# Order of transposes, loads, weight differences and normalisations at the seams of a one-core transformer block

## The chip, the cores and the metric

The kernel runs on one core of a Trainium2 chip. Its engines are TensorE (PE, matrix products; PEld is its weight load), VectorE (DVE), ScalarE (ACT), GpSimd (POOL) and SyncE (SP), whose queue issues nearly all DMAs. The metric is the device time of one execution in microseconds (us), the median of the runs.

## The reference, cut

One block on x (2048 x 1024): a mixer (a recurrent half and a gated half, normalised, times `w_out`), then a feed-forward part with a causal convolution of width 3. Both are wrapped in RMS norms and modulated by six vectors made from c.

```python
mod = c_act @ w_ada[l] + b_ada[l]
sh_m, sc_m, gt_m, sh_f, sc_f, gt_f = split(mod, 6)
h = rmsnorm(x, g_mix_pre) * (1 + sc_m) + sh_m
lru_x, lru_gate, g_u, g_v = split(h @ w_in)
y = concat([rmsnorm(y_lru, g_lru_out), rmsnorm(y_gmlp, g_gmlp_out)])
y = y @ w_out
x = x + gt_m * rmsnorm(y, g_mix_post)
h = rmsnorm(x, g_ffn_pre) * (1 + sc_f) + sh_f
up = causal_depthwise_conv(h @ w_up, ffn_conv_w, ffn_conv_b)
g_ff, v_ff = split(up, 2)
y = (gelu(g_ff) * v_ff) @ w_down
x = x + gt_f * rmsnorm(y, g_ffn_post)
```

## The kernel before

Features lie on the 128 partitions, positions on the free axis. A float32 operand is split into a rounded part (`split`, L136 or L140, a cast) and the rest (L141, a subtraction on DVE); a product is three matmuls of 128x512 (`mm3`, L177 to L179).

**Mixer.** It goes over four chunks of 512 positions: `mixer_z` (products with `w_in`; `v_proj` is its part for `v`), `mixer_norm` (squares on ACT, sums on POOL and DVE, then `rms_bcast`: two matmuls with a matrix of ones, `rl0_m` and `rg0_m` for chunk 0, that add over the partitions; their operand `rl0_hl` is split on DVE), `mixer_out` (product with `w_out`; `oo` is the copy of a result from its bank), `mixer_post`. The vectors of modulation 2 to 5 are made beside it by `ada_task`: DVE sums eight products into `ada_m`, eight transposes on PE turn it, and a reduction on DVE makes a column of each.

**Order.** Background work is written as generators in the list `bg`; each `tick()` in the main loops takes every one a step further, `drain` runs one to its end. A scheduler then orders each engine's instructions by priorities (`tc.high_priority`) and by when tiles come free. Tiles come from pools: `tp` (tag `t4`, 36 tiles), `wp` (`w`, 8), `rw` (`wraw`, 4, raw weights), `lp` (`ld`, 3, loads), `rp` (6). The mixer has its own accumulation banks; those of the feed-forward part, `pf`, take their place when the mixer's last copies are done.

**Feed-forward.** It has two halves C of 1024 positions. `up_phase` runs 24 column blocks f. From f = 2 of C = 0 on, a block is formed from seven products (`up_pair`, `PIECES` 11, t1, t2, 21, 22, t3, t4), each of an operand of `H2` (among them the sums s1 to s4 of four quarters of h, made by `h2_sums`; `hs4` is the split of s4) with a weight piece (a quarter of the block or a difference of quarters). One period of f is 84 matmuls. `up_weights` loads two raw tiles, `wug` and `wuv`, makes the differences on POOL and splits each into a piece; in C = 0 they are also stored to `wkd`, from where C = 1 loads them for f from 2 on. So 22 blocks of C = 0 and two of C = 1 make differences on the chip. `late_chunks` finishes chunks 2 and 3 beside the first up phase. `down(C, t)` multiplies with `w_down` and sums over f in eight banks, one for each d; `evict` squares and copies a bank; `final` normalises with `fr` and adds x2:

```python
t = lp.tile([P, 2, 4, P], F32, tag="ld", name=f"wt{n}")
t2, t1 = t[:, 0], t[:, 1]
w["11"] = piece(b11, f"w11_{n}")
pool.tensor_tensor(out=t1, in0=b12, in1=b11, op=ALU.subtract)
w["t1"] = piece(t1, f"wt1_{n}")
```

`final` of (0,0) runs inside `down(0, 1)`, that of (0,1) at f = 1 of the second up phase, that of (1,0) inside `down(1, 1)`, and that of (1,1) ends the kernel, with its results added to a copy of x2 in DRAM by four accumulating DMAs from POOL.

Of the kernel before, what the change touches and what calls it, by code (L numbers as in the profile page):

```python
# [40 lines left out]
def block_kernel(ctx: ExitStack, tc: tile.TileContext, xt, cols, rows, wada, wada_r, win_k, win_s, win_v, wgate, wsp, wout, wup, wdown, out):  # L41
# [506 lines left out]
    def mixer_out(c, late=False):  # L548
# [690 lines left out]
```

## Time and profile before

| | before |
|---|---|
| median of 3 runs | 2196.03 us (2190.37 to 2196.96) |
| profiled execution | 2193.87 us |
| its span | 2192.1 us |
| mean granted PE clock | 0.975 of full speed |
| PE busy | 2065.3 us, 94% |
| DVE busy | 1427.9 us, 65% |
| ACT busy | 928.2 us, 42% |
| POOL busy | 438.6 us, 20% |
| DMA | 229 GB/s over the span |

The span goes from the first to the last recorded instruction or transfer of the profiled execution; its own time is 1.8 us longer. Busy shares are means over all stages. The idle time in front of an instruction, with what ended it, stands in the timeline in square brackets; a wait counts where the engine that waits is the one the others are waiting for.

### The profile page before, as it was taken

The numbers are of one execution on the slowest core, as the hardware profiler recorded it, in microseconds if no ns is written. First come the engines' busy times: TensorE is split into PE (matmuls) and PEld (weight loads), VectorE is DVE, ScalarE is ACT, GpSimd is POOL, SyncE is SP. The second block draws the span as 40 slices with busy tenths as digits, with TensorE's granted clock in tenths as the row PEclk, the third lists the DMA queues.
The fourth block names the chain that finished last, engine by engine and source line by source line (L and its number), as shares of the span: only waits on it lengthen the run. The fifth ranks groups of instructions, "written<-read, shape, count | busy, mean of one in ns | idle before, by whom it ended". The sixth has DMA issues, their size and how long they took to land.

```text
span 2192.1 us, 24121 instructions
## 1 busy us (share of the span) xinstructions
PE 2065.3 (94%) x9032; PEld 1697.9 (77%) x9032; DVE 1427.9 (65%) x1562; ACT 928.2 (42%) x1198; POOL 438.6 (20%) x252
## 2 busy tenths in 40 slices
PE   5898979999997999999999999989999999999995
PEld 3686868878776887787888878868888888888884
DVE  6787799695765889889877557374444444533634
ACT  3473733543634555555554344243333233422421
POOL 3454244233211425334410000010000000000000
PEclk9999989999998999999999999989999999999997
DMA  8587578577584678898885637547666666444542
GB/s 319 180 319 276 187 272 296 209 276 274 181 296 157 251 280 317 311 322 310 310 295 191 218 124 238 163 169 244 216 224 223 221 221 222 149 158 144 187 146 52
DMA packets 157701, 501.15 MB, mean 229 GB/s; under 512 B 15248, under 2 KB 15376, under 8 KB 157584
## 3 DMA queue, kind: packets, MB, share of 16 engines
q1 hardware_dynamic: 148432, 468.15, 61.8%
q0 software_dynamic: 8000, 27.27, 3.6%
q10 hardware_dynamic: 1152, 4.19, 0.5%
q8 instruction: 71, 1.16, 0.2%
q14 instruction: 46, 0.38, 0.0%
HBM read 343.31 MB, written 158.33 MB: 229 GB/s over the span
## 4 chain that ended last, share of the span: by engine, by line
PE 43%; issue 36%; DVE 12%; DMA 4%; ACT 3%; POOL 1%; SPq 0%; POOLq 0%; DVEq 0%; ACTq 0%
PE dn L177 4%; PE dn L178 4%; PE dn L179 4%; PE upa L972 3%; PE upa L974 3%; PE upa L973 3%; PE upc L972 2%; PE upc L974 2%; PE upc L973 1%; PE lg L177 1%; PE lg L178 1%; PE lg L179 1%; DVE acc L642 1%; PE v L424 1%; PE v L425 1%
## 5 line engine op out<-in xcount | busy, mean ns | idle before, releaser
L177 PE MATMUL dn<-gh,wd_h 128*128 128x512 f32 x768 | 297.1, 390 | 2.5 <-ACT fr_r L202 1.6
L178 PE MATMUL dn<-gl,wd_h 128*128 128x512 f32 x768 | 296.6, 389 | 0.0
L179 PE MATMUL dn<-gh,wd_l 128*128 128x512 f32 x768 | 266.7, 389 | 0.0
L141 DVE TENSOR_TENSOR wd_l<-wd_r,wd_h 128x1024 fp32r<-128x1024 f32 x96 | 117.9, 1230 | 213.3 <-ACT wd_h L136 208.6
L136 ACT CAST wd_h<-wd_r 128x1024 fp32r<-128x1024 f32 x96 | 101.2, 1057 | 284.7 <-PE dn L178 274.1
L919 DVE SCALAR_TENSOR_TENSOR a<-Rg,prm,a 128x1023 f32<-128x1023 f32 x92 | 130.8, 1422 | 132.1 <-ACT a L917 132.1
L177 PEld LDWEIGHTS dn<-gh,wd_h 128*128 128x128 f32 x768 | 144.1, 188 | 34.8 <-ACT wd_h L136 2.6
L179 PEld LDWEIGHTS dn<-gh,wd_l 128*128 128x128 f32 x768 | 144.1, 188 | 30.1 <-DVE wd_l L141 0.2
L178 PEld LDWEIGHTS dn<-gl,wd_h 128*128 128x128 f32 x768 | 144.2, 188 | 29.8
L919 DVE SCALAR_TENSOR_TENSOR a<-Rv,prm,a 128x1023 f32<-128x1023 f32 x92 | 129.6, 1409 | 37.2 <-ACT a L917 36.8
L1120 POOL DMA_DIRECT2D out_dram<-fo x4 | 5.0, 1296 | 711.9 <-DVE fo L1118 709.2
L952 POOL TENSOR_TENSOR wt<-wuv,wug 128x512 f32<-128x512 f32 x24 | 39.0, 1626 | 491.9 <-DMA wuv<-in_wup_dram 377.6
L917 ACT ACTIVATE a<-Rv,prm 128x1024 f32<-128x1024 f32 x46 | 57.3, 1245 | 141.6 <-DVE Rv L1021 141.3
L977 ACT ACTIVATE a<-a 128x1024 f32<-128x1024 f32 x48 | 51.0, 1062 | 68.6 <-DVE a L919 36.8
L136 ACT CAST wt<-wt 128x512 fp32r<-128x512 f32 x72 | 44.7, 621 | 80.0 <-PE upa L974 25.7
L141 DVE TENSOR_TENSOR wt<-wt,wt 128x512 fp32r<-128x512 f32 x72 | 62.1, 864 | 13.9 <-ACT wt L136 13.8
L1021 DVE TENSOR_TENSOR Rv<-upa,m 128x512 f32<-128x512 f32 x46 | 31.5, 686 | 52.9 <-PE upa L974 52.9
L141 DVE TENSOR_TENSOR gl<-gr,gh 128x1024 fp32r<-128x1024 f32 x48 | 58.5, 1219 | 11.4 <-PE upa L974 6.3
L978 DVE TENSOR_TENSOR a<-a,a 128x1024 f32<-128x1024 f32 x48 | 60.5, 1260 | 4.3 <-ACT a L977 4.3
L960 POOL TENSOR_TENSOR wt<-wug,wt 128x512 f32<-128x512 f32 x24 | 42.0, 1750 | 102.6 <-DVE wt L141 83.2
L917 ACT ACTIVATE a<-Rg,prm 128x1024 f32<-128x1024 f32 x46 | 57.1, 1241 | 1.2
L219 POOL TENSOR_TENSOR rp_s<-rp_s,rp_s 128x1024 f32<-128x1024 f32 x12 | 33.0, 2754 | 118.5 <-ACT rp_s L215 118.4
(584 smaller groups left out, 5768.6 us busy)
## 6 DMA issues: line engine op xcount, KB each, us to landing
wd_r<-in_wdown_dram SPq DMA_DIRECT2D x96, 512.0 KB, 4.2
wkd<-wt SPq DMA_DIRECT2D x88, 512.0 KB, 4.4
wkd<-w SPq DMA_DIRECT2D x66, 512.0 KB, 4.2
w<-wkd SPq DMA_DIRECT2D x66, 512.0 KB, 4.3
gd<-a SPq DMA_DIRECT2D x48, 512.0 KB, 3.8
gr<-gd SPq DMA_DIRECT2D x48, 512.0 KB, 3.8
wrt<-wkd SPq DMA_DIRECT2D x44, 512.0 KB, 4.3
wt<-wkd SPq DMA_DIRECT2D x44, 512.0 KB, 4.6
```

The source lines that it names most:

```text
L136: act.copy(out=hi, in_=src)
L141: (leng or vec).tensor_tensor(out=lo, in0=src, in1=hi.bitcast(F32), op=ALU.subtract)
L177: pe.matmul(out=out, lhsT=wh, rhs=mh, start=first, stop=False)
L178: pe.matmul(out=out, lhsT=wh, rhs=ml, start=False, stop=False)
L179: pe.matmul(out=out, lhsT=wl, rhs=mh, start=False, stop=last)
L917: act.activation(out=a, in_=R, func=AF.Identity, scale=w[2], bias=col("ffn_conv_b", blk))
L919: vec.scalar_tensor_tensor(out=a[:, s:], in0=R[:, :FT - s], scalar=w[t], in1=a[:, s:], op0=ALU.mult, op1=ALU.add)
L972: pe.matmul(out=pt, lhsT=wh, rhs=mh, start=first and not more and k == 0, stop=False, skip_group_check=more)
L973: pe.matmul(out=pt, lhsT=wh, rhs=ml, start=False, stop=False, skip_group_check=more)
L974: pe.matmul(out=pt, lhsT=wl, rhs=mh, start=False, stop=last and k == 3, skip_group_check=more)
L977: act.activation(out=g, in_=g, func=AF.Gelu_apprx_tanh)
L978: vec.tensor_tensor(out=g, in0=g, in1=v, op=ALU.mult)
```

## The change

- `ada_task` writes all eight transposes, then the reduction: one of eight columns where the mixer's banks are used, two of four where `pf` is.
- `mixer_norm(0, 4)`: the matmuls of chunk 0's norm come two ticks later.
- In the mixer's last two chunks the copy `oo` has a higher priority, and `h2_sums` from the store loads its last operand `a12` at its start, into a tile of `t4`.
- The weight differences overwrite `wug` and `wuv`; the tile `wt` of the pool `lp` is gone, and POOL's operations and the splits stand in another order.
- The last `down` works off its last four f, not two, d by d, with operands in `t4`; of the four output parts two are added to x2 on DVE and stored by SP, two go through the accumulating DMA.
- The result of `down(0, 1)` is stored to `od`; its `final` starts at f = 3 of the second up phase, a step for each f, and loads each part back.

```diff
@@ ada_task
-        for q in range(2):
-            pt = pts[q].rearrange("p (b c) -> p b c", c=P)
-            for kb in range(4):
-                pe.transpose(out=pt[:, kb], in_=acc[:, 4 * q + kb], identity=ident)
-            vec.tensor_reduce(out=o[:, 4 * q:4 * q + 4], in_=pt, axis=mybir.AxisListType.X, op=ALU.add)
+        n = 8 // len(pts)
+        for kb in range(8):
+            pe.transpose(out=pts[kb // n][:, kb % n], in_=acc[:, kb], identity=ident)
+        for q, pt in enumerate(pts):
+            vec.tensor_reduce(out=o[:, n * q:n * q + n], in_=pt, axis=mybir.AxisListType.X, op=ALU.add)
@@ mixer_out
-            act.copy(out=o, in_=pt)
+            with tc.high_priority(offset=60 if late else 0):
+                act.copy(out=o, in_=pt)
...
-        nt = start(mixer_norm(0) if c == 1 else norm_split(c - 1))
+        nt = start(mixer_norm(0, 4) if c == 1 else norm_split(c - 1))
@@ h2_sums
         if plain:
             put(C, i, "22", a22)
+        else:
+            a12 = get(0, i + 2, "12", True)
...
-        a12 = get(0, i + 2, "12")
         if plain:
+            a12 = get(0, i + 2, "12")
             put(C, i, "12", a12)
-        yield
+            yield
@@ up_weights
-            t = lp.tile([P, 2, 4, P], F32, tag="ld", name=f"wt{n}")
-            t2, t1 = t[:, 0], t[:, 1]
             w["11"] = piece(b11, f"w11_{n}")
-            pool.tensor_tensor(out=t1, in0=b12, in1=b11, op=ALU.subtract)
-            w["t1"] = piece(t1, f"wt1_{n}")
-            pool.tensor_tensor(out=t2, in0=b22, in1=t1, op=ALU.subtract)
-            w["t2"] = piece(t2, f"wt2_{n}")
+            pool.tensor_tensor(out=b11, in0=b12, in1=b11, op=ALU.subtract)
+            w["t1"] = piece(b11, f"wt1_{n}")
+            pool.tensor_tensor(out=b12, in0=b22, in1=b12, op=ALU.subtract)
             w["21"] = piece(b21, f"w21_{n}")
-            pool.tensor_tensor(out=b12, in0=b22, in1=b12, op=ALU.subtract)
+            pool.tensor_tensor(out=b11, in0=b22, in1=b11, op=ALU.subtract)
+            w["t2"] = piece(b11, f"wt2_{n}")
             w["22"] = piece(b22, f"w22_{n}")
             w["t3"] = piece(b12, f"wt3_{n}")
-            pool.tensor_tensor(out=t2, in0=b21, in1=t2, op=ALU.subtract)
-            w["t4"] = piece(t2, f"wt4_{n}")
+            pool.tensor_tensor(out=b21, in0=b21, in1=b11, op=ALU.subtract)
+            w["t4"] = piece(b21, f"wt4_{n}")
@@ down
+        end = C == NFC - 1 and t == 1
+        by_dram = C == 0 and t == 1
+        last_f = 4 if end else 2
...
+            if by_dram and d % 2:
+                sync.dma_start(out=od[:, d - 1:d + 1], in_=O[-1])
...
-        for f in range(2, NF - 2):
+        for f in range(2, NF - last_f):
...
         for d in range(8):
-            for f in range(NF - 2, NF):
+            for f in range(NF - last_f, NF):
                 mm(f, d)
             evict(d)
             tick()
...
-            copied = sync.dma_start(out=out[C, :, :, sl], in_=x2d[C, :, :, sl])
+            copied = sync.dma_start(out=out[C, :, :4, sl], in_=x2d[C, :, :4, sl])
+            X = []
+            for j in range(2):
+                X.append(t4(f"fx{n}_{j}"))
+                sync.dma_start(out=X[j], in_=x2d[C, :, 4 + 2 * j:6 + 2 * j, sl])
@@ final
+                if by_dram:
+                    O[j] = t4(f"fo{n}_{j}")
+                    sync.dma_start(out=O[j], in_=od[:, 2 * j:2 * j + 2])
+                if end and j > 1:
+                    xr = X[j - 2]
...
-                if end:
+                if end and j < 2:
                     add = pool.dma_start(out=out[C, :, 2 * j:2 * j + 2, sl], in_=O[j], accum_op=ALU.add)
...
-    up_phase(1, 0, lambda f: [drain(done.pop(0)) for _ in done[:]] if f == 1 else None)
+    up_phase(1, 0, lambda f: start(done.pop(0)) if f == 3 else None)
+    drain()
```

The scheduler moves instructions with it; three places follow, each as the engine executes it. The number behind a name is its copy, L its line in that kernel's file, and the last word the size.

DVE around the transposes of `ada_m2`, in the product of chunk 0 with `w_out` (`rl1_s0` and `rg1_s0` are the sums of squares of chunk 1, `x2lo` parts of h of chunk 2). Before, from the row behind the first reduction:

```order
L223 TENSOR_TENSOR rl1_s0_1944<-rl1_s0_1944 128x512
L257 SCALAR_TENSOR_TENSOR x2lo2_2043<-x2_2_2040,modc_103,x2hi2_2042 128x512
L140 CAST rl1_hl_2051<-rl1_s0_1944 128x512
L257 SCALAR_TENSOR_TENSOR x2lo2_2043<-x2_2_2040,modc_103,x2hi2_2042 128x512
L223 TENSOR_TENSOR rg1_s0_1993<-rg1_s0_1993 128x512
L141 TENSOR_TENSOR rl1_hl_2051<-rl1_s0_1944,rl1_hl_2051 128x512
L277 SCALAR_TENSOR_TENSOR ada_m3_1930<-wada_3_2_2154,cact_101,ada_m3_1930 128x1024
L286 TENSOR_REDUCE modc_103<-adaps_m2_2092 128x4
L140 CAST rg1_hl_2055<-rg1_s0_1993 128x512
L257 SCALAR_TENSOR_TENSOR x2lo3_2107<-x2_3_2104,modc_103,x2hi3_2106 128x512 x2
L287 TENSOR_TENSOR modc_103<-modc_103,prm_81 128x8
L141 TENSOR_TENSOR rg1_hl_2055<-rg1_s0_1993,rg1_hl_2055 128x512
```

and with the change, from the reduction on:

```order
L289 TENSOR_REDUCE modc_103<-adaps_m2_2092 128x8
L290 TENSOR_TENSOR modc_103<-modc_103,prm_81 128x8
L832 TENSOR_TENSOR gm_105<-modc_103,prm_81 128x8
L223 TENSOR_TENSOR rl1_s0_1944<-rl1_s0_1944 128x512
L257 SCALAR_TENSOR_TENSOR x2lo2_2043<-x2_2_2040,modc_103,x2hi2_2042 128x512
L140 CAST rl1_hl_2051<-rl1_s0_1944 128x512
L257 SCALAR_TENSOR_TENSOR x2lo2_2043<-x2_2_2040,modc_103,x2hi2_2042 128x512
L141 TENSOR_TENSOR rl1_hl_2051<-rl1_s0_1944,rl1_hl_2051 128x512
L277 SCALAR_TENSOR_TENSOR ada_m3_1930<-wada_3_2_2153,cact_101,ada_m3_1930 128x1024
L223 TENSOR_TENSOR rg1_s0_1993<-rg1_s0_1993 128x512
L140 CAST rg1_hl_2055<-rg1_s0_1993 128x512
L141 TENSOR_TENSOR rg1_hl_2055<-rg1_s0_1993,rg1_hl_2055 128x512
```

There is one reduction, ahead of everything; both `x2lo3` fall behind `rg1_hl`, and `rg1_s0` behind `ada_m3`. On PE the eight transposes stand where the first four stood, 48 matmuls ahead of `rl1_m` and `rg1_m`, which now follow each other without the 15 matmuls that parted the halves of `rg1_m`. On POOL the addition for `rg1_s0` comes after the subtraction for `wout0_3_1_l` and a DMA issue, not before them; the next addition, `rp0_s0`, needs a square that ACT makes behind `rl1_r` and `rg1_r`.

ACT at the end of the mixer (`hs2` to `hs4` are the splits of the sums s2 to s4, `w11`, `w21` pieces of f = 1, `oo3_3` the last copy). Before:

```order
L560 COPY oo3_1_4635<-o3_1_4549 128x1024
L136 CAST w11_0_1_4951<-wug0_1_4941 128x512
L136 CAST w21_0_1_4954<-wug0_1_4941 128x512
L215 ACTIVATE rp3_s1_4637<-oo3_1_4635 128x1024
L136 CAST hs3_00h_4671<-hs0011_4589 128x1024
L560 COPY oo3_2_4705<-o3_2_4641 128x1024
L215 ACTIVATE rp3_s2_4707<-oo3_2_4705 128x1024
L136 CAST hs4_00h_4741<-hs0012_4703 128x1024
L560 COPY oo3_3_4773<-o3_3_4711 128x1024
L215 ACTIVATE rp3_s3_4775<-oo3_3_4773 128x1024
```

and with the change:

```order
L136 CAST hs2_00h_4631<-hs0022_4490 128x1024
L136 CAST w22_0_1_4951<-wuv0_1_4945 128x512
L564 COPY oo3_1_4635<-o3_1_4549 128x1024
L215 ACTIVATE rp3_s1_4637<-oo3_1_4635 128x1024
L136 CAST hs3_00h_4671<-hs0011_4589 128x1024
L136 CAST hs4_00h_4704<-hs0012_4492 128x1024
L136 CAST w11_0_1_4954<-wug0_1_4944 128x512
L136 CAST w21_0_1_4957<-wug0_1_4944 128x512
L564 COPY oo3_2_4708<-o3_2_4641 128x1024
L215 ACTIVATE rp3_s2_4710<-oo3_2_4708 128x1024
L564 COPY oo3_3_4771<-o3_3_4714 128x1024
L215 ACTIVATE rp3_s3_4773<-oo3_3_4771 128x1024
```

The cast of `hs4` moves ahead of `w11`, `w21` and the last two copies; `w12` and `w22` stand in this stretch now, where they came ahead of `xf0122` before.

DVE in the second up phase, with the final of (0,1) (`fo01`, `fx01`) among the work of f = 0. Before:

```order
L203 RECIPROCAL fr01_r_10457<-fr01_r_10457 128x512
L1118 SCALAR_TENSOR_TENSOR fo01_0_10252<-fo01_0_10252,gf_107,fr01_r_10457 128x512 x2
L1118 SCALAR_TENSOR_TENSOR fo01_2_10272<-fo01_2_10272,gf_107,fr01_r_10457 128x512
L1021 TENSOR_TENSOR Rv1_0_10407<-upa1_0_10362,m51_0_10390 128x512
L1118 SCALAR_TENSOR_TENSOR fo01_2_10272<-fo01_2_10272,gf_107,fr01_r_10457 128x512
L1118 SCALAR_TENSOR_TENSOR fo01_4_10293<-fo01_4_10293,gf_107,fr01_r_10457 128x512 x2
L1118 SCALAR_TENSOR_TENSOR fo01_6_10314<-fo01_6_10314,gf_107,fr01_r_10457 128x512 x2
L1123 TENSOR_TENSOR fo01_0_10252<-fo01_0_10252,fx01_0_10460 128x1024
L1123 TENSOR_TENSOR fo01_2_10272<-fo01_2_10272,fx01_1_10466 128x1024
L919 SCALAR_TENSOR_TENSOR a1_24_10448<-Rv1_0_10407,prm_81,a1_24_10448 128x1023
```

and with the change, among the convolution of f = 4, the first of four like it:

```order
L926 SCALAR_TENSOR_TENSOR a1_28_10960<-Rv1_4_10919,prm_81,a1_28_10960 128x1022
L931 SCALAR_TENSOR_TENSOR a1_28_10960<-ftails_4093,prm_81,a1_28_10960 128x2
L1140 SCALAR_TENSOR_TENSOR fo01_0_10966<-fo01_0_10966,gf_107,fr01_r_10835 128x512 x2
L1145 TENSOR_TENSOR fo01_0_10966<-fo01_0_10966,fx01_0_10968 128x1024
L926 SCALAR_TENSOR_TENSOR a1_4_11031<-Rg1_4_10918,prm_81,a1_4_11031 128x1023
L931 SCALAR_TENSOR_TENSOR a1_4_11031<-ftails_4093,prm_81,a1_4_11031 128x1
L926 SCALAR_TENSOR_TENSOR a1_4_11031<-Rg1_4_10918,prm_81,a1_4_11031 128x1022
L931 SCALAR_TENSOR_TENSOR a1_4_11031<-ftails_4093,prm_81,a1_4_11031 128x2
```

Before, all eight multiplications and four additions stand together ahead of the convolutions of f = 0; now each f from 4 to 7 has two multiplications and an addition between its two convolutions. On PE `fr01_m` moves 265 matmuls further back.

## Rows read from the trace of the kernel before

**Rows 1.** The page: its first line, the span.
```profile
span 2192.1 us, 24121 instructions
```

**Rows 2.** Windows of 20 us: length, each engine's busy us (xcount), PEclk, DMA share, GB/s.
```profile
1020.00:1040.00 20.00, 17.24 (x70) 13.79 (x69) 17.61 (x21) 11.93 (x20) 3.59 (x2) 0.91 0.89 318
1440.00:1460.00 20.00, 12.05 (x49) 8.73 (x47) 17.59 (x17) 5.63 (x8) 5.13 (x3) 0.88 0.26 81
1460.00:1480.00 20.00, 18.55 (x66) 14.58 (x67) 13.27 (x17) 6.19 (x9) 3.78 (x2) 0.78 0.87 309
1500.00:1520.00 20.00, 20.00 (x90) 16.57 (x89) 9.65 (x15) 6.50 (x8) 0.00 (x0) 1.00 0.65 214
```

**Rows 3.** Waits of PE: operation, line, releaser: us in total, times, longest.
```profile
PE up L972 <- ACT oo L560: 12.4, 1, 12.4
...
PE upc L972 <- ACT wt L136: 5.5, 1, 5.5
PE fr_m L199 <- DVE fr_hl L140: 5.3, 1, 5.3
```

**Rows 4.** Timeline of PE, 195 to 208 us: start, us, line, operation, [idle before].
```profile
199.10 0.76 PE L199 MATMUL rl_m<-rl_hl,onesD 128*128 128x512 f32 x1 [7.40 <-DVE rl_hl L140]
199.66 0.63 PE L424 MATMUL v<-winv_l,x1hi 128*128 128x512 f32 x1
...
202.22 0.48 PE L424 MATMUL v<-winv_l,x1hi 128*128 128x512 f32 x1
...
206.56 0.50 PE L199 MATMUL rl_m<-rl_hl,onesD 128*128 128x512 f32 x1 [2.24 <-DVE rl_hl L141]
```

**Rows 5.** Timeline of PE, 296 to 321 us.
```profile
308.74 1.12 PE L285 MATMUL adaps_m<-ident,ada_m 128*128 128x128 f32 x4 [13.04 <-DVE modc L286]
...
316.99 0.39 PE L177 MATMUL o<-rl0h,wout_h 128*128 128x512 f32 x1
```

**Rows 6.** Timeline of DVE, 296 to 321 us.
```profile
299.65 8.44 DVE L257 SCALAR_TENSOR_TENSOR x2lo<-x,modc,x2hi 128x512 fp32r<-128x512 f32 x2
...
308.61 2.93 DVE L223 TENSOR_TENSOR rl_s<-rl_s 128x512 f32<-128x512 f32 x1
...
316.46 1.41 DVE L257 SCALAR_TENSOR_TENSOR x2lo<-x,modc,x2hi 128x512 fp32r<-128x512 f32 x2
...
317.86 0.68 DVE L141 TENSOR_TENSOR rg_hl<-rg_s,rg_hl 128x512 fp32r<-128x512 f32 x1
```

**Rows 7.** Timeline of POOL, 296 to 321 us: first and last of three operations in a row.
```profile
300.58 2.36 POOL L219 TENSOR_TENSOR rl_s<-rl_s,rl_s 128x1024 f32<-128x1024 f32 x1
...
305.20 2.34 POOL L141 TENSOR_TENSOR wout_l<-wout_r,wout_h 128x1024 fp32r<-128x1024 f32 x1
```

**Rows 8.** Timeline of ACT, 670 to 687 us.
```profile
682.83 1.04 ACT L136 CAST hs_00h<-hs 128x1024 fp32r<-128x1024 f32 x1 [3.60 <-DVE hs L888]
683.78 1.01 ACT L560 COPY oo<-o 128x1024 f32<-128x1024 f32 x1
```

**Rows 9.** Timeline of DVE, 670 to 687 us.
```profile
679.82 2.98 DVE L888 TENSOR_TENSOR hs<-hs,hs 128x1024 f32<-128x1024 f32 x1 [3.67 <-DMA hs<-hs]
```

**Rows 10.** The page, costliest groups: busy us, mean ns of one, idle before and releaser.
```profile
L960 POOL TENSOR_TENSOR wt<-wug,wt 128x512 f32<-128x512 f32 x24 | 42.0, 1750 | 102.6 <-DVE wt L141 83.2
```

**Rows 11.** Timeline of POOL, 1436 to 1468 us.
```profile
1454.79 2.24 POOL L952 TENSOR_TENSOR wt<-wuv,wug 128x512 f32<-128x512 f32 x1 [29.43 <-DVE fo L1123]
```

**Rows 12.** Timeline of DVE, 1555 to 1570 us.
```profile
1564.75 1.28 DVE L919 SCALAR_TENSOR_TENSOR a<-Rg,prm,a 128x1023 f32<-128x1023 f32 x1 [5.32 <-ACT a L917]
```

**Rows 13.** Timeline of DVE, 2158 to 2193 us.
```profile
2169.01 0.69 DVE L141 TENSOR_TENSOR fr_hl<-fs,fr_hl 128x512 fp32r<-128x512 f32 x1
...
2174.76 5.39 DVE L1118 SCALAR_TENSOR_TENSOR fo<-fo,gf,fr_r 128x512 f32<-128x512 f32 x8
```

**Rows 14.** DMA issues by tile: count, KB each, median us from issue to landing.
```profile
out_dram<-fo SPq DMA_DIRECT2D x12, 512.0 KB, 4.4
```

**Rows 15.** Timeline of POOL, 2158 to 2193 us.
```profile
2183.20 1.22 POOL L1120 DMA_DIRECT2D out_dram<-fo  x1 [2.69 <-issue]
```

More of the change, by code (lines that the diff above doesn't have):

```diff
@@ L280, in ada_task @@
         o = modv[:, m]
-        pts = [bank(f"adaps_m{m}_{q}") for q in range(2)] if banks else psum(f"adaps_m{m}").rearrange("p q c -> q p c")
-        for q in range(2):
-            pt = pts[q].rearrange("p (b c) -> p b c", c=P)
-            for kb in range(4):
-                pe.transpose(out=pt[:, kb], in_=acc[:, 4 * q + kb], identity=ident)
-            vec.tensor_reduce(out=o[:, 4 * q:4 * q + 4], in_=pt, axis=mybir.AxisListType.X, op=ALU.add)
+        if banks:
+            pts = [bank(f"adaps_m{m}_{q}").rearrange("p (b c) -> p b c", c=P) for q in range(2)]
+        else:
+            pts = [psum(f"adaps_m{m}").rearrange("p q (b c) -> p (q b) c", c=P)]
+        n = 8 // len(pts)
[3 more added lines that the diff above has]
+            vec.tensor_reduce(out=o[:, n * q:n * q + n], in_=pt, axis=mybir.AxisListType.X, op=ALU.add)
         vec.tensor_tensor(out=o, in0=o, in1=bav[:, m], op=ALU.add)
@@ L869, in h2_sums @@
             put(C, i, "22", a22)
+        else:
+            a12 = get(0, i + 2, "12", True)
         yield
@@ L891, in from_store, with get @@
     def from_store(C, i):
-        def get(t, j, o):
-            x = lp.tile([P, 2, 512], F32, tag="ld", name=f"hs{C}{i}{o}")
+        def get(t, j, o, other=False):
+            n = f"hs{C}{i}{o}"
+            x = t4(n) if other else lp.tile([P, 2, 512], F32, tag="ld", name=n)
             sync.dma_start(out=x, in_=hs[C, i, ("11", "12", "21", "22").index(o)])
@@ L1042, in block_kernel @@
     done = []
+    od = dram.tile([P, ND, 512], F32, name="od")
     def down(C, t):
@@ L1055, in operands @@
                     sync.dma_start(out=raw, in_=gd[C, :, f:f + 2, sl])
-                    hl = [wp.tile([P, 2, 512], F32R, tag="w", name=f"g{q}{n}_{f}") for q in "hl"]
+                    if f >= NF - last_f and end:
+                        hl = [h4(f"g{q}{n}_{f}") for q in "hl"]
+                    else:
+                        hl = [wp.tile([P, 2, 512], F32R, tag="w", name=f"g{q}{n}_{f}") for q in "hl"]
                     split(hl[0], hl[1], raw, "act")
@@ L1059, in operands @@
                     G[f + b] = hl[0][:, b], hl[1][:, b]
-            W[f] = weight(wdown[f], [P, 8, P], f"wd{n}_{f}", ahead=150)
+            W[f] = weight(wdown[f], [P, 8, P], f"wd{n}_{f}", ahead=150, mk=h_like if f >= NF - last_f and end else None)
         def mm(f, d):
@@ L1068, in down @@
         O, acc = [], []
-        end = C == NFC - 1 and t == 1
         def evict(d):
@@ L1097, in down @@
             tick()
-        for f in range(NF - 2, NF):
+        for f in range(NF - last_f, NF):
             operands(f)
         for d in range(8):
-            for f in range(NF - 2, NF):
+            for f in range(NF - last_f, NF):
                 mm(f, d)
@@ L1112, in final @@
             for j in range(4):
-                if not end:
+                if by_dram:
[3 more added lines that the diff above has]
+                    xr = X[j - 2]
+                elif not end:
                     xr = lp.tile([P, 2, 512], F32, tag="ld", name=f"fx{n}_{j}")
```

## The prediction

> **What bounds the kernel now.** I read the page first, for the span [rows 1], then the waits of TensorE (PE), then windows of 20 us, then the timelines of single engines around each wait. PE is the bound: in a stretch without a wait it issues 90 matmuls in 20.00 us [rows 2], which is 0.222 us for one, with nothing idle. So the time can only fall where PE stands still or runs at the lower clock. The waits list [rows 3] names the places that the change touches: 12.4 us for the copy `oo` at the end of the mixer, 5.5 us for a weight difference `wt` early in the second up phase, 5.3 us for `fr_hl` at the very end; two more, at 199 us for `rl_hl` [rows 4] and at 308 us for `modc` [rows 5], are shown as timeline rows. A wait has a second price: PE comes back at the lower clock. After the wait that ended at 199.10 seven matmuls start from 199.66 to 202.22 [rows 4], 0.43 us apart, twice the normal spacing; that is the 1.2 GHz level. I therefore cost a place by missing matmuls or by when PE reaches the same instruction, not by the wait alone.
>
> **Part by part.** All gains are against the profiled execution, 2193.87 us; the median of the three runs is 2196.03, 2.2 us above it.
>
> *Norm of chunk 0 two ticks later.* PE stopped at 199.10 - 7.40 = 191.7, came back for the first half of `rl_m`, did the 14 `v` matmuls up to 204.3 and stopped again for the second half until 206.56 [rows 4]. Now 17 `v` matmuls go first (3.8 us, to 195.5) and then both halves want the same split that ended at 206.5; nothing in the order of DVE makes that earlier. Three more matmuls are done by then, +0.7 us. But the slow restart, which before lay between the two waits and cost nothing, now lies behind the last one: 8 matmuls with 0.2 us too much, -1.6. Sum -1 us. Bounds: -3 if the split comes somewhat later, +1 if the clock holds.
>
> *All eight transposes first.* PE stopped at 308.74 - 13.04 = 295.7 [rows 5] because the second four transposes wait for the reduction of the first four (their bank is one tile), and DVE was held by `x2lo`: two of them took 8.44 us, where two later ones took 1.41 [rows 6]. They overlap three POOL operations in a row, from 300.58 to 307.54 [rows 7]. Now PE need not wait there; it runs 25 more matmuls, to 301.3, and then meets `rl1_m` and `rg1_m`, whose splits were ready only at 317.86 + 0.68 = 318.5 [rows 6]. Before, PE began the matmul behind them at 316.99 [rows 5], since the last half of `rg1_m` stood 15 matmuls further on. So the wait is not removed; what counts is when `rg1_hl` is ready now. From the end of `x2lo` (308.1) to that split DVE took 10.4 us. In the new order two `x2lo` (1.41) come after it, and the 2.93 us of `rl_s` [rows 6], which a POOL addition had held, shrink to about 0.7, since that addition now stands behind `rl1_r`. That leaves about 7 us: 315 if `x2lo` ends where it did, 312 if it slips in at the DMA issue that now parts POOL's operations (305.2). I take 314; with the four small matmuls and a slow restart of 1.3 us PE is then where it was at 316.99, or 0.7 us ahead: +1 us. Bounds: -4 (split at 318.5 and a new slow restart behind it), +4 (split at 311). The Trainium skill (SBUF — State Buffer, Who interferes with whom) says that a VectorE instruction with two SBUF inputs and a GpSimd instruction that reads SBUF exclude each other, and the one that comes second is blocked until the other is done; the 8.44 against 1.41 agrees. By that rule `x2lo`, which still meets the same three POOL operations, would stay blocked to their end, this part would be about -1 instead of +1, and the sum 2 us smaller.
>
> *Copy of `oo` ahead, `a12` loaded early.* PE stopped at 684.84 - 12.37 = 672.5 by the waits [rows 3, 8]: its new banks wait for the last copy, `oo3_3`, 683.78 to 684.79 [rows 8]. ACT stood idle for 3.60 us just before the cast of `s4`, which is queued ahead of that copy [rows 8]; DVE's subtraction for it had waited 3.67 us for the load and then took 2.98 [rows 9]. With the load in a tile of the large pool, far ahead, the idle time goes and ACT's work stays: 684.79 - 3.60 = 681.2. The ring of three load slots has one load less in its chain, so the operands ahead of it come up to 3 us earlier too. I take +4 us, bounds +1 (ACT waits for another operand instead) and +7.
>
> *Weight differences in place.* The same four POOL operations for each f, 1.75 us each in the dearest group [rows 10]; but now each that overwrites a tile waits for the split of its former content, so POOL can't run ahead. The chain for one f is three operations and the splits between them: with 1.75 us for each of the three and as much for each split, 10.5 us, within a period of 84 matmuls, 18.7 us. As the pieces' slots come free about a period ahead of use, this is hidden: 0 us. If the cover were gone it would cost in each of 24 f's. Two stretches in which the late chunks are finished lose matmuls, 20 of 90 in the second [rows 2], 4.4 us; they have no `wt` wait in them and keep their order, so I leave them. Bounds: +9 if both go, -6 if they grow.
>
> *First half's last normalisation.* In 1440 to 1480 us PE issued 49 + 66 of 180 matmuls [rows 2]: 65 missing, 14.4 us. POOL's first difference of f = 1 had waited 29.43 us until 1454.79 for `fo` [rows 11], since its tile shares the load slots with `fx` and DVE's whole final of (0,1) stands ahead of it. Both go: the difference needs no slot, and the final is spread over four later f's. There DVE idles 5.32 us in each period [rows 12]; a share of the final is two operations of 0.67 (5.39 for eight [rows 13]) and one addition, at most the 2.98 of the one in [rows 9]: 4.3 us, covered if the reload of `fo` has landed. If it has not, DVE's work behind waits, at most the 4.4 us of a DMA [rows 14] each time. The eight transfers more on SP's queue (512 KB each) and the waiting stores hold back weights that are loaded more than a period ahead. I take +12, bounds +8 and +14.4.
>
> *The end.* PE waited 5.3 us from its last `dn` matmul to the split of `fr` [rows 3]: evictions were behind, because each d had only 6 matmuls (1.3 us). With 12 (2.7 us) they keep up, and what follows the last matmul is four operations of about 0.69 [rows 13], 2.7 us: +2.6. From the first multiplication (2174.76 [rows 13]) to the end of the span (2192.1 [rows 1]) took 17.3 us; POOL issued the last accumulating DMA at 2183.20 [rows 15], 8.9 us before the end. Now two of the four parts go that way: second part ready at 2.7, a queued issue of 1.2, 8.9: 12.8 us. The other two: 5.4 for the multiplications, twice 1.35 for the additions (by their size twice 0.67), 4.4 for the store [rows 14]: 12.5 us. With 0.4 of issue, 13.2 in place of 17.3: +4. Together +6.5, bounds +4 and +9.
>
> **Sum.** -1 + 1 + 4 + 0 + 12 + 6.5 = 22.5 us: 2171.4. I forecast 2172 us for the median, since the runs shown lie on both sides of the profiled one.
>
> **Rivals.** *The seams' waits only move.* DVE is held beside POOL as before, the splits come no earlier: -3, -4 and +1 for the first three parts, the rest as above: gain 12.5, 2181 us. The operations of [rows 6, 7] all remain, which speaks for it; against it, POOL's additions stand further apart in the new order. 20%. The port rule of the Trainium skill (SBUF — State Buffer, Who interferes with whom) is on this rival's side.
>
> *More goes than I count.* The two stretches of the late chunks fill too (+8.9), as load slots are free and POOL's operations are spread out, and the splits come early (+2.6): 2160 us. Against it: their loads keep their place in SP's queue. 13%.
>
> *The in-place chain starves PE* (slower). Place: each f whose differences are made on the chip, 24 of them. POOL waits for DVE's split, DVE is held by POOL, and a piece comes late. It decides at 22.5 / 24 = 0.94 us for each f; at 2 us it is 2171.4 + 48 = 2219 us. The 1.75 us against a period of 18.7 speak against it; that the last difference already waited 83.2 us in all for a split [rows 10] speaks for it. 6%.
>
> *The reloaded `fo` blocks DVE* in four f's, 4 us each: 2187 us. For it: the load is issued late and DVE takes its work in order. 6%. The forecast itself has 55%.
>
> **Range and chances.** The forecast's own range is 2164 to 2180. With the first rival and most of the second, 2156 to 2184 leaves out about 2 in 10. This measurement tells 0.3%, 6.6 us, from no change, so faster means under 2189.4: forecast, the first two rivals and half of the last, 90%; same 5%; slower 5%.
>
> **What would show it.** The waits list should have no `upc <- wt` row of 5.5 us and the windows from 1440 to 1480 near 90 matmuls; the wait at `up` 7 to 10 us instead of 12.4; one wait of some 11 us at `rl_m`, and one at `rl1_m` or `rg1_m` in place of `adaps`; at the end `fr_m` under 3 us and about 13 us from the first multiplication to the end. Wrong would be: `wt` rows as releasers of PE all through the first up phase, or DVE idle behind a DMA for `fo` with PE waiting for a `R` or `m` tile.

## The result and the profile after

| | before | changed |
|---|---|---|
| median | 2193.69 us (2188.31 to 2196.96, 5 runs) | 2165.65 us (2161.46 to 2170.77, 5 runs) |
| ratio | | 0.9882, 95% interval 0.9866 to 0.9897 |
| span of the profiled execution | 2192.1 us | 2159.7 us |
| mean granted PE clock | 0.975 | 0.98 |

The forecast was 2172 (2156 to 2184). By the medians 28.0 us are gone, by the ratio 25.9, by its interval 22.6 to 29.4. The page of the changed kernel, against [rows 1]:

```profile
span 2159.7 us, 24180 instructions
...
PE 2054.6 (95%) x9032; PEld 1689.3 (78%) x9032; DVE 1418.9 (66%) x1561; ACT 929.9 (43%) x1200; POOL 435.4 (20%) x250
```

PE's waits (operation, line, releaser: us in total, times, longest), against [rows 3]:

```profile
PE rl_m L199 <- DVE rl_hl L140: 14.0, 2, 10.6
PE rl_m L199 <- DVE rl_hl L141: 9.2, 3, 6.9
...
PE up L977 <- ACT oo L564: 7.8, 1, 7.8
...
PE fr_m L199 <- DVE fr_hl L140: 2.6, 1, 2.6
```

The row `upc <- wt` is gone, `up` fell from 12.4 to 7.8 and `fr_m` from 5.3 to 2.6. In place of `adaps` there is a wait of 10.6 us at a second `rl_m`: the wait has moved, not gone. At the first `rl_m`, that of chunk 0, PE waits twice, 3.5 us for L140 and 6.9 for L141, together near the one wait of 11 that the prediction named. The windows say the same (PE's count first, PEclk third from the end), against [rows 2]:

```profile
300.00:320.00 20.00, 9.22 (x29) 6.60 (x30) 19.86 (x20) 7.85 (x9) 7.86 (x6) 0.66 0.77 296
1440.00:1460.00 20.00, 20.00 (x90) 16.57 (x89) 11.04 (x16) 7.70 (x10) 0.00 (x0) 1.00 0.65 215
1460.00:1480.00 20.00, 20.00 (x90) 16.57 (x89) 8.69 (x12) 6.87 (x8) 0.00 (x0) 1.00 0.66 223
```

1440 to 1480 is full, while 300 to 320 holds 29 matmuls (46 before, where PE came to this place 3.4 us later). The places in detail. PE around 308 us, against [rows 5]:

```profile
308.82 0.77 PE L199 MATMUL rl_m<-rl_hl,onesD 128*128 128x512 f32 x1 [10.55 <-DVE rl_hl L140]
310.00 0.80 PE L199 MATMUL rl_m<-rl_hl,onesD 128*128 128x512 f32 x1 [0.41 <-DVE rl_hl L141]
312.34 1.43 PE L199 MATMUL rg_m<-rg_hl,onesD 128*128 128x512 f32 x2 [1.55 <-DVE rg_hl L140]
313.57 0.63 PE L177 MATMUL o<-rl0h,wout_h 128*128 128x512 f32 x1
314.00 0.63 PE L178 MATMUL o<-rl0l,wout_h 128*128 128x512 f32 x1
```

DVE in the same stretch, against [rows 6]:

```profile
298.81 5.41 DVE L253 SCALAR_TENSOR_TENSOR x<-x,sm,n_r 128x512 f32<-128x512 f32 x2 [4.26 <-DMA x<-in_xt_dram]
304.14 1.40 DVE L257 SCALAR_TENSOR_TENSOR x2lo<-x,modc,x2hi 128x512 fp32r<-128x512 f32 x2
305.46 1.21 DVE L289 TENSOR_REDUCE modc<-adaps_m 128x8 f32<-128x1024 f32 x1
...
311.05 0.68 DVE L223 TENSOR_TENSOR rg_s<-rg_s 128x512 f32<-128x512 f32 x1
...
312.23 0.69 DVE L141 TENSOR_TENSOR rg_hl<-rg_s,rg_hl 128x512 fp32r<-128x512 f32 x1
```

and POOL, against [rows 7]:

```profile
295.39 2.42 POOL L219 TENSOR_TENSOR rl_s<-rl_s,rl_s 128x1024 f32<-128x1024 f32 x1
297.75 2.37 POOL L141 TENSOR_TENSOR wout_l<-wout_r,wout_h 128x1024 fp32r<-128x1024 f32 x1
300.05 0.57 POOL L169 DMA_DIRECT2D kept_o<-wout_h  x1
300.64 2.35 POOL L219 TENSOR_TENSOR rg_s<-rg_s,rg_s 128x1024 f32<-128x1024 f32 x1
```

`x2lo` now takes 1.40 us for two, but another pair with two inputs in SBUF, `x`, stands ahead of it: it waited 4.26 us for its load and then took 5.41, ending at 304.2, while POOL was at work until 303.0. `rg_hl` is ready at 312.9, and PE goes on from there at the lower clock: the matmuls behind it start 0.43 us apart (313.57, 314.00).

ACT before the wait at `up` ended (673.3), against [rows 8]:

```profile
667.36 1.98 ACT L136 CAST hs_00h<-hs 128x1024 fp32r<-128x1024 f32 x2
669.24 1.13 ACT L136 CAST w<-wug 128x512 fp32r<-128x512 f32 x2
670.28 1.00 ACT L564 COPY oo<-o 128x1024 f32<-128x1024 f32 x1
671.31 1.06 ACT L215 ACTIVATE rp_s<-oo 128x1024 f32<-128x1024 f32 x1
672.28 0.99 ACT L564 COPY oo<-o 128x1024 f32<-128x1024 f32 x1
```

The idle time is gone: ACT works without a gap up to `oo3_3` (672.28). What is left of this wait is ACT's own queue, with the six instructions above ahead of the copy that PE waits for.

The end on DVE, against [rows 13]:

```profile
2139.29 0.69 DVE L141 TENSOR_TENSOR fr_hl<-fs,fr_hl 128x512 fp32r<-128x512 f32 x1
...
2144.74 5.39 DVE L1140 SCALAR_TENSOR_TENSOR fo<-fo,gf,fr_r 128x512 f32<-128x512 f32 x8
2150.04 2.35 DVE L1145 TENSOR_TENSOR fo<-fo,fx 128x1024 f32<-128x1024 f32 x2
```

and the last two stores on SP:

```profile
2151.29 1.51 SPq L1146 DMA_DIRECT2D out_dram<-fo  x2
```

The multiplications begin 15.0 us before the end of the span; before it was 17.3.

**Stages.** One execution's span differs from another's by several us for reasons that no edit has: `first`, the opening stage, runs the same order in all kernels and its last matmul starts anywhere from 87.5 (the changed kernel) to 93.1 us, at 92.3 in the profiled execution of before. So I compare stages: the time from the start of one matmul to the start of another, each counted within its group in the trace.

- N: last `first` to 49th `lg` (norm of chunk 0)
- T: 49th `lg` to 151st `o` (transposes and `rl1_m`, `rg1_m`)
- S: 441st to 481st `o`, about 585 to 600 us (norm of chunk 3)
- R: 481st to last `o`
- U: last `o` to 31st `up` (the copy `oo`)
- P: 31st `up` to 21st `dn` (first up phase)
- Q: 271st to 341st `upb` (second up phase, about f = 0 to 6)
- L: 341st to last `upb` (the rest of it)
- E: last `upb` to last `fr_m` (the second of the pair, also where a row merges the two); Z: from there to the end of the span

| kernel | N | T | S | R | U | P | Q | L | E | Z |
|---|---|---|---|---|---|---|---|---|---|---|
| before | 122.5 | 103.5 | 14.8 | 71.7 | 22.3 | 470.7 | 131.4 | 325.3 | 278.2 | 22.3 |
| changed | 123.9 | 104.5 | 11.0 | 72.9 | 16.9 | 470.6 | 117.0 | 325.3 | 275.5 | 19.7 |
| g_alone | 122.1 | 104.2 | 14.8 | 71.7 | 19.3 | 472.6 | 117.0 | 325.3 | 278.2 | 22.7 |
| h_alone | 122.1 | 104.2 | 14.8 | 71.6 | 19.5 | 470.6 | 117.0 | 325.3 | 278.2 | 23.5 |
| fx_own | 122.4 | 104.1 | 16.1 | 71.7 | 22.3 | 471.0 | 117.0 | 325.3 | 278.2 | 22.3 |
| f_alone | 122.4 | 104.2 | 16.0 | 71.6 | 18.7 | 471.5 | 131.2 | 325.3 | 278.2 | 22.9 |
| b_alone | 122.5 | 104.1 | 11.0 | 72.6 | 22.2 | 471.5 | 131.2 | 325.3 | 278.2 | 22.7 |
| i_alone | 122.4 | 104.1 | 14.8 | 71.7 | 19.6 | 468.6 | 130.3 | 325.3 | 275.5 | 20.1 |
| i_route | 122.3 | 104.2 | 14.8 | 71.7 | 19.6 | 469.9 | 131.3 | 325.3 | 278.2 | 20.0 |
| no_a | 122.5 | 104.1 | 11.1 | 72.6 | 19.0 | 470.5 | 117.0 | 325.3 | 275.5 | 20.0 |
| no_b | 123.7 | 104.6 | 14.8 | 71.7 | 16.4 | 470.1 | 117.0 | 325.3 | 275.5 | 19.7 |
| no_h | 123.8 | 106.1 | 11.1 | 72.2 | 18.3 | 469.7 | 117.0 | 325.3 | 275.5 | 20.4 |
| no_g | 123.7 | 104.6 | 11.1 | 72.3 | 16.7 | 469.6 | 117.0 | 325.3 | 275.5 | 19.7 |
| vec_sums | 122.3 | 100.7 | 10.2 | 71.7 | 17.1 | 469.5 | 117.0 | 325.3 | 275.5 | 20.3 |

A column whose values fall into two groups by an edit shows that edit (N, S, Q, E, Z); where one kind of kernel spreads by itself, as U does (19.3 to 22.3 without the edit), only the means tell. Two stages lie between those shown. From the 21st `dn` to the 271st `upb` it is 269.7 to 269.8 in all kernels. From the 151st to the 441st `o` it is 264.1 in `vec_sums` and 265.4 to 268.0 in the others, not in two groups by any one edit.

### The profile page after: what moved, and what is told of

Its sections match the earlier page's. It is cut to its first block, busy times and chain, and to the rows that moved or that the text cites. A ratio compares the mean times of both kernels' runs of the same rounds, so it can differ in the third digit from the quotient of the medians.

```text
span 2159.7 us, 24180 instructions
## 1 busy us (share of the span) xinstructions
PE 2054.6 (95%) x9032; PEld 1689.3 (78%) x9032; DVE 1418.9 (66%) x1561; ACT 929.9 (43%) x1200; POOL 435.4 (20%) x250
## 4 chain that ended last, share of the span: by engine, by line
PE 75%; DVE 12%; issue 4%; DMA 4%; ACT 4%; POOL 1%; SPq 0%; DVEq 0%; ACTq 0%; POOLq 0%
PE dn L177 8%; PE dn L178 8%; PE dn L179 8%; PE upa L977 7%; PE upa L979 7%; PE upa L978 7%; PE upc L979 3%; PE upc L978 3%; PE upc L977 3%; PE upb L978 2%; PE upb L979 2%; PE upb L977 2%; DVE acc L646 1%; PE lg L177 1%; PE lg L178 1%
## 5 line engine op out<-in xcount | busy, mean ns | idle before, releaser
L141 DVE TENSOR_TENSOR wd_l<-wd_r,wd_h 128x1024 fp32r<-128x1024 f32 x96 | 117.0, 1223 | 194.4 <-ACT wd_h L136 186.8
L136 ACT CAST wd_h<-wd_r 128x1024 fp32r<-128x1024 f32 x96 | 101.0, 1056 | 275.5 <-PE dn L178 259.8
L957 POOL TENSOR_TENSOR wug<-wuv,wug 128x512 f32<-128x512 f32 x24 | 41.9, 1747 | 520.7 <-DVE w L141 520.7
L141 DVE TENSOR_TENSOR wt<-wug,wt 128x512 fp32r<-128x512 f32 x72 | 72.5, 1007 | 32.7 <-ACT wt L136 32.6
L136 ACT CAST wt<-wug 128x512 fp32r<-128x512 f32 x72 | 44.9, 623 | 98.3 <-POOL wug L957 38.8
L141 DVE TENSOR_TENSOR gl<-gr,gh 128x1024 fp32r<-128x1024 f32 x48 | 58.6, 1220 | 13.7 <-ACT gh L136 7.4
L136 ACT CAST gh<-gr 128x1024 fp32r<-128x1024 f32 x48 | 50.8, 1057 | 12.4 <-DMA gr<-gd 8.7
```

The source lines that it names most:

```text
L136: act.copy(out=hi, in_=src)
L141: (leng or vec).tensor_tensor(out=lo, in0=src, in1=hi.bitcast(F32), op=ALU.subtract)
```

## The experiments

**Who held the second up phase.** `g_alone` is the kernel before with the in-place `up_weights` alone, `h_alone` with `od` and the start of `final` at f = 3 alone (both as in the diff above). `fx_own` has neither:

```diff
-                    xr = lp.tile([P, 2, 512], F32, tag="ld", name=f"fx{n}_{j}")
+                    xr = t4(f"fx{n}_{j}") if C == 0 and t == 1 else lp.tile([P, 2, 512], F32, tag="ld", name=f"fx{n}_{j}")
```

> The kernel before with the in-place weight differences alone (the tile wt of the load pool gone, final of (0,1) still at f = 1). Theory 'slot': the 14.4 us lost between 1440 and 1480 us come from the load slot that wt shares with fx, so this edit alone gains 8 us or more there, and the row upc <- wt of 5.5 us goes. Rival 'DVE': the final of (0,1) on DVE stands ahead of the splits and of Rv, so the edit alone gains at most 3 us there. Both: nothing in the first up phase, 600 to 1160 us, beyond 4 us either way. Total -8 us (slot) or -1 us (DVE). If the in-place chain cost PE anything, it would be slower than before.

> The kernel before with the move of the last normalisation of (0,1) alone (stored to od, started at f = 3, a step for each f; wt still in the load pool). Both theories of the 14.4 us, 'slot' and 'DVE', have fx and the final out of the way of f = 1, so both expect -13 us in all: 90 matmuls in each window from 1440 to 1480, and a loss of 0 to 2 us later, in f = 4 to 7, where the reload stands. The rival 'reload blocks DVE' expects four stalls of about 4 us in f = 4 to 7, so no gain.

> The kernel before with one line changed: the loads fx of the final of (0,1) go into tiles of the large pool, so they don't hold the load slots. Nothing else of the change is in it; the final still stands at f = 1, all at once, and wt keeps its pool. Theory 'slot' (the in-place edit and the moved final both only freed these slots): -12 to -14 us, no row upc <- wt, the stage from f = 0 to f = 6 of the second up phase 14 us shorter, as with either edit. Rival 'the new order of the differences' or 'the final spread over four f': -4 us or less, since neither is in it.

Measured: ratio 0.9944 (0.9925 to 0.9963), 0.9945 (0.9925 to 0.9964) and 0.9946 (0.9927 to 0.9965). All three take stage Q from 131.4 to 117.0, to the tenth the 14.4 us that were missing. The windows of `fx_own`:

```profile
1440.00:1460.00 20.00, 20.00 (x90) 16.54 (x89) 16.30 (x21) 5.44 (x9) 2.21 (x1) 1.00 0.60 215
1460.00:1480.00 20.00, 20.00 (x90) 16.57 (x89) 12.18 (x15) 7.08 (x9) 0.00 (x0) 1.00 0.95 324
```

its POOL, whose first difference of f = 1 starts 29 us earlier than the row of [rows 11]:

```profile
1425.41 1.30 POOL L952 TENSOR_TENSOR wt<-wuv,wug 128x512 f32<-128x512 f32 x1 [4.76 <-issue]
```

and its DVE:

```profile
1452.68 5.38 DVE L1118 SCALAR_TENSOR_TENSOR fo<-fo,gf,fr_r 128x512 f32<-128x512 f32 x8
```

The final's eight multiplications still stand in one piece in the middle of f = 0 and 1, and PE issues 90 matmuls in each window beside them. So the theory "slot" holds: `fx` held the load slot that `wt` needed, and no part of the stall was the final's place on DVE. "DVE" falls. The reload of `fo` lies in Q and L, and both are the same with it (`h_alone`) and without it (`g_alone`, `fx_own`): "reload blocks DVE" falls as well, at a price of 0.0 us.

`no_h` and `no_g` are the changed kernel with the one or the other undone.

> The changed kernel with the final of (0,1) back at f = 1, without od. As the in-place differences alone took 12.3 us off and the moved final alone 12.4 us, each should do nearly the work of both: 0 to 3 us slower than the changed kernel (ratio 0.988 to 0.990), a stall of at most 3 us near 1420 us. Rival 'they add up': 12 us slower, ratio 0.994.

> The changed kernel with the weight differences in their own tile of the load pool again (the final stays at f = 3). By my step the in-place form costs and brings nothing in the first up phase: equal to the changed kernel within 2 us, ratio 0.987 to 0.989. Rival 'in-place chain costs': this kernel is faster by 3 us or more. Rival 'slots for the late chunks': slower by 3 us or more, as the loads of late_post and h2_sums share three slots with wt again.

Measured: 0.9885 (0.9861 to 0.9909) and 0.9876 (0.9856 to 0.9896), neither to be told from 0.9882. With both edits in place either can go. In the first up phase P is 469.5 to 472.6 with the in-place differences and 468.6 to 471.5 without them: no cost and no gain shows there, and both rivals of `no_g` fall. The two stretches of the late chunks did not fill: P, in which they lie, is 470.7 before and 470.6 changed.

**The copy of `oo`.** `f_alone` is the kernel before with the priority and the early `a12`.

> The kernel before with the early load of a12 and the higher priority of the copy oo alone. Expected: the wait at up falls from 12.4 to about 7.8 us and PE reaches that instruction 5 us earlier. Besides, in the changed kernel PE gained 3.7 us between 417 and 640 us, where no edit was made that I had costed: if the higher priority of oo or the new load order does that, it is seen here, total -8 to -9 us; if it is due to another edit or to the single execution, total -5 us.

Measured: 0.9991 (0.9980 to 1.0002), that is 2.0 us (-0.4 to 4.4), less than the 5 that I expected and not clear of zero. Its waits:

```profile
PE up L976 <- ACT oo L561: 8.5, 1, 8.5
...
PE upc L976 <- ACT wt L136: 5.5, 1, 5.5
```

and the same wait in `g_alone`, which lacks the edit:

```profile
PE up L970 <- ACT oo L560: 9.8, 1, 9.8
```

The wait at `up` is not 12.4 us in each execution of the old code: stage U is 22.3, 22.3 and 22.2 in three kernels without the edit and 19.3 to 19.6 in four. With the edit it is 16.4 to 19.0. The means, 20.7 and 17.6, make the edit worth 3.1 us, though four of the seven kernels with it also have the later norm of chunk 0 (16.4 to 18.3; the other three 17.1 to 19.0), and whether that has a part in it was not separated. Of the 5.4 that the profiled pair shows, the rest lies within the spread of the old code. Why the old code has two levels here stays open. The gain near 590 us is not from this edit (S 16.0).

**Transposes.** `b_alone` has the eight transposes ahead of the sum and nothing else; `no_b` is the changed kernel with the old order of them.

> The kernel before with the eight transposes first, alone. Theory 'm4': the stage around 590 us (from the 441st to the 481st matmul of the products with w_out) takes 11.0 in place of 14.8 us, and about 1 us of it is given back by 672 us; the stage at 308 us is no shorter (0 to 1 us longer), its wait at rl_m and rg_m. Total -2 to -3 us. Rival 'chance': the stage at 590 us stays at 14.8 us, total 0.

> The changed kernel with the transposes back in two halves, each ahead of its sum. My step: the wait at 308 us only moves, so nothing there (0 to 1 us). Theory 'm4': the single sum spares DVE a late instruction in the third such place too (556 us), and that is why rg_m of chunk 3 waited 0.6 in place of 2.6 us and PE gained 3 us between 590 and 600 us; then this kernel is 3 us slower than the changed one, with a wait of 2.6 us back at rg_m. Rival: that gain is from another edit or from the execution, and this kernel equals the changed one within 1 us.

Measured: `b_alone` 0.9997 (0.9986 to 1.0009), `no_b` 0.9891 (0.9870 to 0.9911). `no_b` waits as before does, in both places:

```profile
PE adaps_m L285 <- DVE modc L286: 13.1, 1, 13.1
...
PE rg_m L199 <- DVE rg_hl L140: 2.6, 1, 2.6
```

Stage T doesn't feel the edit: 104.1 in `b_alone` and `no_a`, 103.5 to 104.2 in the kernels with neither this edit nor the later norm. Stage S does: 11.0 to 11.1 in each kernel with the edit (10.2 in `vec_sums`), 14.8 or more in each without. "m4" holds, and the rows show by which way. DVE, before and in `b_alone`:

```profile
579.50 4.89 DVE L852 SCALAR_TENSOR_TENSOR xf<-xf,sf,rq_r 128x512 f32<-128x512 f32 x4
...
577.47 3.96 DVE L855 SCALAR_TENSOR_TENSOR xf<-xf,sf,rq_r 128x512 f32<-128x512 f32 x6
```

and PE behind the split of `rg_hl`, before and in `b_alone`:

```profile
593.46 0.47 PE L199 MATMUL rg_m<-rg_hl,onesD 128*128 128x512 f32 x1 [2.56 <-DVE rg_hl L140]
594.92 0.61 PE L178 MATMUL o<-rl2l,wout_h 128*128 128x512 f32 x1
...
592.20 0.47 PE L199 MATMUL rg_m<-rg_hl,onesD 128*128 128x512 f32 x1 [0.56 <-DVE rg_hl L140]
```

In `b_alone` the vector `sf` is made before the reciprocal of 3.32 us, not behind it, and six `xf` go in one piece before POOL's addition for `rl_s` (582.17 in `b_alone`). Before, four of them meet that addition (581.00 to 583.84) and take 4.89 us, the operand `uu` behind them comes later, and with it the squares, their addition and the split of `rg_hl`. There PE waits 2.0 us longer, and then eight matmuls start 0.43 us apart (594.92 to 598.32), which `b_alone` doesn't have. All eight kernels with the old order have the four `xf` at 4.87 to 4.89 us, but no run moves `xf` alone.

About 0.9 us is given back in R. Alone the edit brings 0.7 us by the time (-2.0 to 3.1), less than the 2 to 3 that I expected; the 2.9 of the stages lie within the interval. The wait at the copy of `oo` stays as it was before (12.0 and 12.4 us):

```profile
PE up L975 <- ACT oo L563: 12.0, 1, 12.0
```

There ACT's 3.60 us of idle time behind the load of `a12` are still there. Whether the edit needs the copy's edit beside it to shorten the whole is not shown. From the times alone, 0.9891 against 0.9882, its gain could not be shown; it rests on the stages.

**Norm of chunk 0.** `no_a` is the changed kernel with `mixer_norm(0)` as before.

> The changed kernel with the norm of chunk 0 back at its old place (two ticks earlier). My step: the later place costs 1 us, since a slow restart comes behind the last wait; in the profiled pair it cost 1.3 us. So this kernel is 1 us faster than the changed one, ratio to before about 0.9877 where the changed kernel had 0.9882. Rival 'the later place pays elsewhere', in an order that the traces of one execution don't tell apart: 1 to 3 us slower.

Measured: 0.9881 (0.9865 to 0.9898). The time doesn't tell it, the stage does: N is 123.7 to 123.9 in the four kernels with the later place and 122.1 to 122.5 in the ten without. The edit costs 1.4 us there. PE at chunk 0's norm in the changed kernel, against [rows 4]:

```profile
194.18 0.47 PE L199 MATMUL rl_m<-rl_hl,onesD 128*128 128x512 f32 x1 [3.46 <-DVE rl_hl L140]
201.59 0.79 PE L199 MATMUL rl_m<-rl_hl,onesD 128*128 128x512 f32 x1 [6.94 <-DVE rl_hl L141]
```

Behind the second wait nine matmuls start 0.43 us apart (202.18 to 206.02); in [rows 4] such a stretch lies between the two waits. T doesn't give it back (104.5 to 106.1 in those four); the stage behind T and stage U spread too much to tell.

**The end.** `i_alone` has the whole new end, `i_route` only the routing of the four parts (the diff's lines on `copied`, `X` and `j`).

> The kernel before with the new end alone (last four f worked off by d, two output parts added on DVE and stored by SP). Expected: fr_m waits 2.6 in place of 5.3 us, and from the first multiplication to the end about 13.5 in place of 17.3 us: total -7 us. Rival: the two edits share one chain (the copy of x2 and the DMAs), so only one of the two counts: -3 to -4 us.

> The kernel before with only the routing of the last four output parts changed (two added on DVE and stored by SP), while the last two f are worked off by d as before. Theory 'two separate gains': from the first multiplication to the end about 15.0 in place of 17.3 us, fr_m still waits 5.3 us: -2 to -3 us. Rival 'one chain': either edit alone gives the whole 5.5 us or nothing.

Measured: 0.9967 (0.9952 to 0.9981) and 0.9975 (0.9963 to 0.9988). `i_route` waits for `fr` as before:

```profile
PE fr_m L199 <- DVE fr_hl L140: 5.3, 1, 5.3
```

E is 278.2 with the routing alone and 275.5 with the whole, Z is 20.0 and 20.1 against 22.3 (22.3 to 23.5 in the kernels with the old end, 22.7 in the mean). Two gains: 2.7 for working off four f by d, as much as the wait at `fr_m` fell, and by the means 2.7 for the routing. By the time `i_route` gained 5.5 us (2.6 to 8.1), so its stage lies at the lower edge of the interval; why its middle lies higher is open.

**A further step.** The wait at `rl1_m` and the one at `rg_m` of chunk 3 both end with splits that wait for additions on POOL or are held beside them. `vec_sums` is `no_a` with one more line in `norm_scale`:

```diff
-            qs.append(SumSq(name))
+            qs.append(SumSq(name, vec))
```

> The changed kernel with the norm of chunk 0 back at its old place and with the additions of the squares of the mixer's two norms on DVE, not on POOL. Theory 'POOL holds DVE and is itself late': the splits of rl1 and rg1 come 3 us earlier, rg_s of chunk 3 no longer waits 2.3 us for POOL; with the 1.4 us of the old place that is 4 to 6 us faster than the changed kernel: ratio to before 0.985 to 0.986. Rival 'DVE is full at these places': the eight additions more on DVE (1.2 us each) delay the same splits, and it is equal to the changed kernel or up to 4 us slower.

Measured: 2155.83 us (2153.77 to 2157.75), ratio 0.9835 (0.9817 to 0.9853): faster than both kernels, and by its median by more than I expected (0.985 to 0.986). PE at `rl1_m`:

```profile
307.56 0.76 PE L199 MATMUL rl_m<-rl_hl,onesD 128*128 128x512 f32 x1 [8.50 <-DVE rl_hl L140]
309.06 0.80 PE L199 MATMUL rl_m<-rl_hl,onesD 128*128 128x512 f32 x1 [0.74 <-DVE rl_hl L141]
```

and DVE:

```profile
296.83 1.22 DVE L219 TENSOR_TENSOR rl_s<-rl_s,rl_s 128x1024 f32<-128x1024 f32 x1
...
302.02 1.21 DVE L219 TENSOR_TENSOR rg_s<-rg_s,rg_s 128x1024 f32<-128x1024 f32 x1
...
309.59 0.68 DVE L141 TENSOR_TENSOR rg_hl<-rg_s,rg_hl 128x512 fp32r<-128x512 f32 x1
```

An addition takes 1.2 us here and 2.4 on POOL, and it no longer stands beside DVE's other work. The split of `rg1` ends at 310.3, from a start no earlier than in the changed kernel; T falls to 100.7, S to 10.2, R to 71.7, and N is back at 122.3. Against `no_a` the largest gain, nearly 4 us, is in the stage between T and S (264.1 and 268.0), where the norm of chunk 2 lies. "DVE is full" falls. How much is due to the shorter additions and how much to DVE no longer being held was not separated.

## Why the prediction was right, and where its terms were off

| part | forecast | stages |
|---|---|---|
| norm of chunk 0 later | -1 | -1.4 (N) |
| transposes, at 308 us | +1 | 0 (T) |
| transposes, near 590 us | not counted | +2.9 (S 3.8, R -0.9) |
| copy of `oo`, early `a12` | +4 | +3.1 (U) |
| differences in place, first up phase | 0 | 0 (P) |
| second up phase | +12 | +14.4 (Q) |
| the end | +6.5 | +5.4 (E 2.7, Z 2.7 by the means) |
| sum | 22.5 | 24.4 |

The sum of the stages lies in the interval of the time, 22.6 to 29.4 us; the ratio's 25.9 is 1.5 above it and the median's 28.0 is 3.6, of which the luck of the opening stage may be a part; that was not tried. That the forecast sum is so near is in part luck: 5.3 us that it left out or held back stand against 3.4 that it counted too much. A small slip of reading: in a full stretch matmuls start 0.227 us apart in the trace, not the 0.222 that 90 in 20 us gives, since a window also counts a matmul that reaches into it.

- *Norm of chunk 0*: right in kind and nearly in size. Both halves wait for the split that came at the same place of DVE's order, and the slow restart is on the path.
- *Transposes at 308*: right that the wait moves to `rl1_m` and `rg1_m`. I took `rg1_hl` to gain some 4 us, and it gained less. With this edit alone (`b_alone`) POOL's operations keep their order, `x2lo` is held as long as before, and a product of 3.40 us for `ada_m` comes ahead of the second half of the split:

```profile
299.49 8.49 DVE L257 SCALAR_TENSOR_TENSOR x2lo<-x,modc,x2hi 128x512 fp32r<-128x512 f32 x2
...
320.64 0.68 DVE L141 TENSOR_TENSOR rg_hl<-rg_s,rg_hl 128x512 fp32r<-128x512 f32 x1
```

In the four kernels with the later norm, one of them without this edit (`no_b`), `x` with its late load and two inputs in SBUF took the place of `x2lo` beside POOL (5.41 to 5.82 us for two). The rule of the Trainium skill that I weighed (SBUF — State Buffer, Who interferes with whom), by which this part would have been -1, came as near as my +1, and the 8.49 us agree with it. `vec_sums` fits the rule's direction: without POOL's additions the same stage is 3.4 us shorter than in `no_a`, part of which is the shorter additions themselves.
- *The step that failed*: I costed the transposes at one of their places. `ada_task` runs for m = 3 and 4 as well, where PE doesn't wait at the transposes, so I left them out. But for m = 4 the edit reorders DVE ahead of chunk 3's norm, and a wait 30 us later is shorter (`rg_m`, 2.6 to 0.6 us, and the slow restart behind it), by way of `sf` and `xf` as the rows of `b_alone` show.
- *Copy of `oo`*: right mechanism; I took the wait of one execution, at the upper of its two levels, for the kernel's.
- *In place*: right, 0, and the slower rival did not come.
- *Second up phase*: the 14.4 us were all there to be had; the 2.4 that I held back for the reload cost nothing. I named two causes, the slot and the final's place on DVE; only the slot counted, and one line frees it.
- *The end*: both gains are there, the first as forecast (2.7 against 2.6), the second smaller (2.7 against 4). The additions ended 7.7 us behind the first multiplication (2152.4), where my sum had 8.1, but the last store took 5.9 us to land, not 4.4 (issued 2152.43, landed 2158.37), and 1.3 us more pass from there to the end of the span, which I had counted for POOL's way and not for SP's: 15.0 us in place of 13.2.

The rival "the waits only move" had the first two waits right, though it priced them too high; "more goes" (2160) lies about as far from the measured 2165.65 as the forecast, on the other side, but its gain of 34 us lies outside the interval, and its way didn't come true: the late chunks' stretches stayed.

## What to carry to other kernels

When a small pool serves two streams, look for the tile that waits for the other stream's consumer: one line in `fx_own` did what two rewrites did. A generator that runs several times is costed at each of its places, also where nothing waits at the place itself, and the instructions behind it are followed to the next wait. Before a wait is booked as a gain, look at it in a second execution, and compare stages rather than spans where an edit is worth a few us.

## What the runs showed of the hardware

Where the code of this place and of all before it was the same (before, `h_alone`, `fx_own`, `i_alone`, `i_route`), PE stopped at `up` for 10.2 to 12.4 us in one execution of each, and the opening stage, the same in all fourteen kernels, varied by 5.6 us. Additions of 128x1024 on POOL took 2.35 to 2.42 us in the rows above, and DVE instructions beside them took three times and more of their usual time (8.49 us in `b_alone` for two `x2lo` that took 1.40 in the changed kernel, where no POOL operation stood beside them); the same additions on DVE took 1.2 us each, and moving them there took the ratio from 0.9881 (`no_a`) to 0.9835.
